# The entry of two feed-forward layers: fewer blocks of eight products, and products of later blocks between the token halves

## The chip, the cores and the metric

The kernel runs on one core of one Trainium2 chip. The metric is the device time of one execution, in microseconds (us). TensorE (PE) multiplies matrices into accumulator banks; VectorE (DVE), ScalarE (ACT) and GpSimd (POOL) work element by element; the transfers from and to HBM run through DMA queues, most of which SyncE (SP) issues. Each engine works through its own instructions in a fixed order and waits on semaphores for what the others write.

## What is computed

One step of a model of two layers, in float32, over 512 latent tokens and 128 prompt tokens. The model width is 1024, the feed-forward width 2816. The layers differ in their mixers (layer 0: two kinds of attention heads side by side, layer 1: grouped-query attention), which the change doesn't touch. What it touches is the second half of each layer:

```
g = silu(condition) @ w_mod[l] + b_mod[l]   # six vectors: shift, scale, gate of mixer and feed-forward
h = rms_norm(x, norm_ffn[l]) * (1 + scale2) + shift2
gate, up = split(h @ w_ffn_in[l])           # 1024 -> 2 x 2816
x = x + gate2 * ((silu(gate) * up) @ w_ffn_out[l])
```

Latent and prompt tokens have a condition each, so that every modulation vector is needed twice.

## The kernel before

**Operands.** The activations lie transposed, features on the 128 partitions and tokens along the free axis. The 640 tokens are two halves of 320: the first is latent, the second has 192 latent tokens and the 128 of the prompt, so that steps which depend on the condition are 192 and 128 wide there. To keep float32 precision, each operand is split into a high part and the rest (on ACT a copy, on DVE or POOL a subtraction), and a product is three matmuls: high by high, high by rest, rest by high (L61 is the line of all of them). A matmul of 128 x 128 by 320 tokens is the unit of this text.

**Feed-forward, first product.** `ffn` goes over 22 blocks of 128 hidden features. A block has a gate and an up matrix, 1024 x 128 each. It is done in one of two ways:

- *Eight products*: gate and up times both token halves, each over eight feature tiles: 2 x 2 x 8 x 3 = 96 matmuls.
- *Seven products*: the two matrices and the two token halves are cut into a 2 x 2 scheme, feature tiles 0 to 3 against 4 to 7 and half against half. With sums of weights (wX, wY, wZ, wW, made for each block, two additions of 512 for `s13` and two for `s24` among them) and sums of tokens (D, N, C, E, made once a layer by `add_up`), seven products of half the depth do the work of eight: 7 x 4 x 3 = 84 matmuls. They accumulate in three banks: fg (X times 11, then N, C, E), fd (D, then 22) and fu (X times 21). Between the products ACT copies a bank aside (p1, p5, u1) and DVE adds one; the last product (E), the SiLU and the multiplication of a block are done in `close`, after the first two products of the next block.

The first `FEW` blocks, five in layer 0 and four in layer 1, are done in the first way. The seven-product loop needs both token halves and their sums, and its weight tiles wr, w4 and ws and the tile cb serve until then as 32-bit room for the tokens (`ModS`). `hidden` splits a block's result, stores it to HBM and loads it again for the second product; the last three blocks stay.

**Second token half.** The mixer's last product adds to x column by column; its normalisation of the second half is postponed and handed to the feed-forward as `pend`, which is called after three feature tiles of block 0. It makes eight tiles h01q (layer 1: h11q) of the second half: a multiplication on DVE (h01t), a scale and shift on ACT (into h0132a, d, u), a copy on ACT (L287) and a subtraction on DVE (L288). PE reduces the squares for the norm in between (oanp, whose input is oanacc, its result oanrs).

**Second product.** It has two passes over the eight output columns n. In each column weights wo are split, PE accumulates fo, and a residual (L313) adds the gated bank to x.

**Modulation beside it.** `mod_side` makes the modulation vectors that come next: for each 128 of them a tile wm of 1024 x 128 is loaded (512 KB), and DVE multiplies it by the SiLU of either condition and sums (two `junk` steps, L1306). The conditions lie broadcast in the tile cb, which is loaded and put through SiLU once a layer. A plan, a function of the step's kind and number, says how many tiles stand behind each block ("fb") and each column ("n") of the second product.

```
side = mod_side([(0, wm0g, G2)] + [(1, wm1[j:j + 8], j) for j in (SH1, SC1, G1, SH2, SC2)],
```

These are 48 tiles in layer 0; layer 1 has the eight of its own gate.

**What sets the order.** A scheduler lays out the instructions of each engine once, when the program is built, from the order of the code and its dependences; `after` ties an instruction behind another one. Raw loads go through three buffers (`raw`, L162) on SP's queue, so that a load waits until the split of three loads before has been made; weights split by `unit` and `split` have three buffers in each of two pools.

## Time and profile before

| | us |
|---|---|
| median of three runs (least, greatest) | 1553.18 (1552.89, 1554.06) |
| span of the profiled execution | 1549.2 |
| PE busy / weight loads | 1485.5 / 1425.0 |
| DVE, ACT, POOL busy | 1109.3, 738.6, 230.0 |

HBM reads are 182.86 MB and writes 28.46 MB. The page and the rows below speak of one profiled execution; the span runs from its first to its last instruction. In a row, `out<-in` are the program's names without numbers, a time in brackets is the idle time of the engine before the instruction with what released it, and in the rows of waits the three numbers are the idle time in all, how often, and the mean. In windows the columns are the stretch, its length, and the busy time of each engine with the number of instructions; PEclk is the granted clock as a share of full speed.

### The profile page before, as it was taken

How to read it: one execution, taken by the hardware profiler on the slowest of the kernel's cores; microseconds unless marked ns; L12 is line 12 of the kernel's file. 1: busy time of each engine (PE TensorE's matmuls, PEld its weight loads, DVE VectorE, ACT ScalarE, POOL GpSimd, SP SyncE). 2: the span in 40 equal slices, each digit the busy share in tenths (PEclk: the TensorE clock that was granted, in tenths of full speed). 3: DMA queues.
4: the chain of work that ended last, by engine and by line, in shares of the span. 5: the costliest groups of instructions: out<-in, count | busy, mean ns of one | idle time of the engine just before them, and what ended most of it. 6: DMA issues, size and time to landing. Idle time of an engine off the chain costs nothing.

```text
span 1549.2 us, 25659 instructions
## 1 busy us (share of the span) xinstructions
PE 1485.5 (96%) x9988; PEld 1425.0 (92%) x9988; DVE 1109.3 (72%) x2071; ACT 738.6 (48%) x1420; POOL 230.0 (15%) x303
## 2 busy tenths in 40 slices
...
GB/s 368 109 96 169 165 140 42 14 53 125 45 210 185 176 173 160 154 238 309 232 219 133 89 41 28 28 15 96 45 199 199 160 133 136 141 219 254 88 41 69
DMA packets 73098, 212.99 MB, mean 137 GB/s; under 512 B 8096, under 2 KB 12976, under 8 KB 72720
## 3 DMA queue, kind: packets, MB, share of 16 engines
...
HBM read 182.86 MB, written 28.46 MB: 136 GB/s over the span
## 4 chain that ended last, share of the span: by engine, by line
PE 78%; DVE 11%; ACT 6%; DMA 3%; issue 2%; POOL 0%; DVEq 0%; ACTq 0%; POOLq 0%
PE fg L61 16%; PE fo L61 10%; PE fd L61 8%; PE fu L61 4%; PE gq L61 2%; PE nk L61 2%; PE nq L61 1%; PE go L61 1%; PE mod L61 1%; PE fo_2b L61 1%; PE fo_4b L61 1%; PE fo_2a L61 1%; PE fo_4a L61 1%; PE fo_6b L61 1%; PE fo_6a L61 1%
## 5 line engine op out<-in xcount | busy, mean ns | idle before, releaser
L1306 DVE SCALAR_TENSOR_TENSOR junk<-wm,cb 128x1024 bf16<-128x1024 f32 x112 | 136.7, 1221 | 25.0 <-DMA wm<-in_wm 11.2
L245 POOL TENSOR_SCALAR h10h<-h10t,gs,mods 128x320 fp32r<-128x320 f32 x4 | 5.5, 1386 | 438.9 <-DVE h10t L239 436.9
L61 PE MATMUL gq<-h10h,wgq 128*128 128x320 f32 x256 | 66.4, 318 | 0.2
L61 PE MATMUL fg<-h01q,wgu 128*128 128x320 f32 x240 | 50.2, 319 | 0.9 <-DVE h01q L288 0.4
L1069 ACT ACTIVATE wY<-s 128x1024 fp32r<-128x1024 f32 x35 | 37.1, 1060 | 23.6 <-PE fg L61 20.2
L1069 ACT ACTIVATE wZ<-s 128x1024 fp32r<-128x1024 f32 x35 | 37.1, 1060 | 23.4 <-PE fd L61 15.8
L1138 DVE TENSOR_TENSOR sg<-up,sg 128x640 f32<-128x640 f32 x35 | 28.8, 822 | 25.2 <-ACT sg L1137 25.2
L61 PEld LDWEIGHTS gq<-h10h,wgq 128*128 128x128 f32 x256 | 45.3, 190 | 1.4 <-PE gtp L65 0.6
L1070 DVE TENSOR_TENSOR wZ<-s,wZ 128x1024 fp32r<-128x1024 f32 x35 | 42.7, 1221 | 2.3
L1070 DVE TENSOR_TENSOR wY<-s,wY 128x1024 fp32r<-128x1024 f32 x35 | 42.7, 1219 | 0.5 <-ACT wY L1069 0.3
L313 DVE SCALAR_TENSOR_TENSOR xr<-fo,mods,xr 128x320 f32<-128x320 f32 (+2 forms) x48 | 19.6, 436 | 32.2 <-PE fo L61 32.0
L61 PEld LDWEIGHTS fg<-h01q,wgu 128*128 128x128 f32 x240 | 38.7, 190 | 3.6 <-DVE h01q L288 2.1
L61 PE MATMUL fg<-h11q,wgu 128*128 128x320 f32 x192 | 40.6, 320 | 0.9 <-DVE h11q L288 0.4
L1476 ACT ACTIVATE gp<-gs,gb,rq 128x640 f32<-128x640 f32 (+1 forms) x40 | 31.9, 797 | 19.2 <-DVE gb L1475 17.1
L61 PE MATMUL gq<-h10l,wgq 128*128 128x320 f32 x128 | 39.7, 310 | 0.0
L1137 ACT ACTIVATE sg<-fg 128x320 f32<-128x320 f32 x35 | 15.3, 438 | 46.7 <-PE fg L61 46.7
L61 PE MATMUL fg<-h11E,wW 128*128 128x320 f32 x216 | 34.7, 309 | 0.0
L61 PE MATMUL fd<-h11q,wZ 128*128 128x320 f32 x216 | 34.6, 309 | 0.0
L61 PE MATMUL fg<-h11q,wX 128*128 128x320 f32 x216 | 34.6, 309 | 0.0
L1171 ACT ACTIVATE p<-fd 128x320 f32<-128x320 f32 x35 | 15.3, 438 | 40.4 <-PE fd L61 40.3
L61 PE MATMUL fg<-h11N,wZ 128*128 128x320 f32 x216 | 34.6, 309 | 0.0
L61 PE MATMUL fu<-h11q,wX 128*128 128x320 f32 x216 | 34.6, 309 | 0.0
...
## 6 DMA issues: line engine op xcount, KB each, us to landing
wm<-in_wm SPq DMA_DIRECT2D x48, 512.0 KB, 4.2
mraw<-in_wm SPq DMA_DIRECT2D x24, 512.0 KB, 3.6
...
wm<-in_wm0g SPq DMA_DIRECT2D x8, 512.0 KB, 5.0
...
```

Source lines behind the costliest of these rows:

```text
L61: cls.last = nc.tensor.matmul(*a, **k)
L245: G.tensor_scalar(h[:, c0:c1], t, self.gsl[:, k, 0:1], self.ml[:, self.sh + k, 0:1], ALU.mult, ALU.add)
L313: V.scalar_tensor_tensor(xo[:, c0:c1], ps[:, c0 - o:c1 - o], ml[:, g + n, c:c + 1], xi[:, c0:c1], ALU.mult, ALU.add)
L1069: S.activation(t[:, 0, :], src, AF.Copy)
L1070: V.tensor_tensor(t[:, 1, :], src, f(t[:, 0, :]), ALU.subtract)
L1137: last = S.activation(sg[:, 0:HT], g[:, :HT], AF.Silu, scale=-1.0)
L1138: V.tensor_tensor(sg, up, sg, ALU.mult)
L1171: S.activation(p5, b5[:, :HT], AF.Copy)
L1306: V.scalar_tensor_tensor(junk, raw, 1.0, cb[:, c, :], ALU.mult, ALU.mult, accum_out=mods[l][:, j0 + i, c:c + 1])
L1476: S.activation(dst, src, AF.Exp, bias=nb, scale=rq[:, j:j + 1], accum_out=ll[:, j:j + 1])
```

## The change

- `FEW` is 2 in both layers: blocks 2, 3 and (in layer 0) 4 are done by seven products.
- `AHEAD` = 2: the first two products with wX (X times 11 and X times 21, which need only the first token half) of blocks 2 and 3 stand between block 0's first and second token half. Their sum lies in a tile p1 until the block is closed, and their gate bank stays open for N, C and E. wX_2 is loaded and split in `pre`, in the mixer's tail.
- Blocks 0 and 1 take their banks half by half, gate from one kind and up from the other, and are gated half by half. `add_up` has the first two of its four parts before the early product of block 3.
- The second half's 32-bit room takes the two w4 tiles in place of four u tiles.
- `mod_side` starts after block 1. Its load of the conditions goes through SP's queue rather than ACT's, and the SiLU is two steps of 1024, placed at block 2's close.
- The plans: layer 0 has tiles behind the blocks 6 to 21 apart from 10, 15 and 20 (13 tiles), and the second product 35 (before 16 and 32). Layer 1 has its eight tiles behind blocks 6 to 13 (before 2 to 9).

```diff
-    FEW = 5, 4
+    FEW = 2
+    AHEAD = 2
...
+            w.append(unit(wFI[l, FEW, 1], 1024, f"wX{l}_{FEW}", pool=fp))
...
+        def ahead(fb, wX):
+            g, b2, up = bank(f"fg{l}_{fb}"), bank(f"fu{l}_{fb}", "y"), utile(f"p1{l}_{fb}")
+            product(g, wX, 0, 11, True)
+            S.activation(up, g[:, :HT], AF.Copy)
+            product(b2, wX, 512, 21, True)
+            V.tensor_tensor(up, b2[:, :HT], up, ALU.add)
+            early[fb] = g, up
+
+        eight(0, w0, 0, range(3))
+        pend()
+        eight(0, w0, 0, range(3, KT))
+        wX = [w0[2]]
+        ahead(FEW, wX[0])
+        wX += [unit(wFI[l, FEW + i, 1], 1024, f"wX{l}_{FEW + i}") for i in range(1, AHEAD)]
+        w1 = [unit(wFI[l, 1, i], 1024, f"wgu{l}_1{i}") for i in range(2)]
+        sg = tmp(f"sg{l}_0")
+        gated(sg, 0)
+        for k in range(2):
+            hm.add_up(k)
+        for i in range(1, AHEAD):
+            ahead(FEW + i, wX[i])
+        eight(0, w0, 1)
...
+        step = side(fk)
...
-            after(gate, lambda: S.activation(cb, cb, AF.Silu))
...
+                if (kind, at) == ("fb", FEW):
+                    for c in range(2):
+                        S.activation(cb[:, c, :], cb[:, c, :], AF.Silu)
...
-                    lambda kind, i: (0, 0, 0, 2, 3)[i] if kind == "fb" and i < 5 else int(i % 3 > 0) if kind == "fb" else (0, 1, 1, 1, 2, 2, 2, 2, 3, 3, 3, 3, 2, 3, 2, 2)[i])
+                    lambda kind, i: int(i > 5 and i % 5 > 0) if kind == "fb" else (1, 2, 2, 2, 2, 2, 2, 2, 3, 3, 3, 3, 2, 2, 2, 2)[i])
...
-    side = mod_side([(1, wm1[G2:], G2)], lambda kind, i: int(kind == "n" or i > 1))
+    side = mod_side([(1, wm1[G2:], G2)], lambda kind, i: int(kind == "n" or i > 5))
```

**PE at the seam of the token halves, layer 0.** fg0_00 and fu0_0a are block 0's gate and up bank of the first half, h01q70 the last feature tile of that half and h01q01 the first of the second. Before:

```order
L61 MATMUL fg0_00_4883<-h01q60_4748,wgu0_0_4705 128x320 x3
L61 MATMUL fu0_0a_4885<-h01q60_4748,wgu0_1_4710 128x320 x3
L61 MATMUL fg0_00_4883<-h01q70_4749,wgu0_0_4705 128x320 x3
L61 MATMUL fu0_0a_4885<-h01q70_4749,wgu0_1_4710 128x320 x3
L61 MATMUL fg0_01_4884<-h01q01_4750,wgu0_0_4705 128x320
L61 MATMUL fu0_0b_4886<-h01q01_4750,wgu0_1_4710 128x320
```

Now (of each four feature tiles the first and the last row):

```order
L61 MATMUL fg0_00_4886<-h01q70_4752,wgu0_0_4705 128x320 x3
L61 MATMUL fu0_00_4887<-h01q70_4752,wgu0_1_4710 128x320 x3
L61 MATMUL fg0_2_4988<-h01q00_4745,wX0_2_4715 128x320 x3
...
L61 MATMUL fg0_2_4988<-h01q30_4748,wX0_2_4715 128x320 x3
L61 MATMUL fu0_2_4989<-h01q40_4749,wX0_2_4715 128x320 x3
...
L61 MATMUL fu0_2_4989<-h01q70_4752,wX0_2_4715 128x320 x3
L61 MATMUL fg0_3_5061<-h01q00_4745,wX0_3_5019 128x320 x3
...
L61 MATMUL fg0_3_5061<-h01q30_4748,wX0_3_5019 128x320 x3
L61 MATMUL fu0_3_5062<-h01q40_4749,wX0_3_5019 128x320 x3
...
L61 MATMUL fu0_3_5062<-h01q70_4752,wX0_3_5019 128x320 x3
L61 MATMUL fg0_01_5090<-h01q01_4753,wgu0_0_4705 128x320 x3
L61 MATMUL fu0_01_5091<-h01q01_4753,wgu0_1_4710 128x320 x3
```

The second half's first use stands 48 matmuls later, behind the banks fg0_2, fu0_2, fg0_3 and fu0_3.

**ACT between blocks 1 and 3, layer 0.** h01E3 is the last token sum, sg a gate's SiLU, hd0_0h the copy that a store takes, wW to wZ are splits. Before:

```order
L306 ACTIVATE h01E3_4773<-h0132d0_4736 128x320
L1294 DMA cb_4957<-in_crow 128x2048
L1122 ACTIVATE sg0_1_5211<-fg0_11_5086 128x320
L170 ACTIVATE wgu0_21_5233<-wgu0_21r_5231 128x1024
L1090 ACTIVATE hd0_0h_4251<-sg0_1_5211 128x640
L1295 ACTIVATE cb_4957<-cb_4957 128x2048
L1122 ACTIVATE sg0_2_5332<-fg0_20_5222 128x320
L170 ACTIVATE wgu0_30_5349<-wgu0_30r_5347 128x1024
```

Now:

```order
L306 ACTIVATE h01E3_4776<-h0132d0_4741 128x320
L1185 ACTIVATE wW0_2_5295<-wg0_2r_5293 128x512
L1185 ACTIVATE wW0_3_5373<-wg0_3r_5371 128x512
L1092 ACTIVATE hd0_0h_4251<-sg0_0_5032 128x640
L1336 ACTIVATE cb_5285<-cb_5285 128x1024
L1114 ACTIVATE sg0_1_5224<-fg0_11_5227 128x320
L1336 ACTIVATE cb_5285<-cb_5285 128x1024
L1092 ACTIVATE hd0_0h_4251<-sg0_1_5224 128x640
L1206 ACTIVATE p50_2_5313<-fd0_2_5310 128x320
L1071 ACTIVATE wY0_3_5379<-s130_3_5376 128x1024
L1071 ACTIVATE wX0_4_5474<-wu0_4r_5470 128x1024
L1210 ACTIVATE u10_2_5314<-fg0_2_4988 128x320
```

The load of cb has left ACT's queue, and both halves of its SiLU stand ahead of hd0_0h's second copy and of p50_2, the copy of bank fd that block 2's next product into fd waits for. On SP's queue the load stands here:

```order
L162 DMA wu0_4r_5470<-in_wFI 128x1024
L1180 DMA wg0_3r_5371<-in_wFI 128x1024
L1330 DMA cb_5285<-in_crow 128x2048
L1098 DMA sp0_0h_5170<-hd0_0h_4251 128x640
L1098 DMA sp0_0l_5172<-hd0_0l_4252 128x640
L1180 DMA wg0_4r_5472<-in_wFI 128x1024
```

It is ahead of block 0's two stores and of the loads for block 4.

**DVE at columns 3 and 4 of layer 0's second product, first pass.** xr is a column of x, wo0_0_40 and wo0_0_45 are the two weight splits of column 4, junk the modulation. Before:

```order
L313 SCALAR_TENSOR_TENSOR xr3_4486<-fo0_0_30_7965,mods0_98,xr3_4486 128x320
L1306 SCALAR_TENSOR_TENSOR junk1110_8308,mods1_99<-wm1_11_8306,cb_4957 128x1024
L1306 SCALAR_TENSOR_TENSOR junk1111_8310,mods1_99<-wm1_11_8306,cb_4957 128x1024
L313 SCALAR_TENSOR_TENSOR xr3_4486<-fo0_0_31_7966,mods0_98,xr3_4486 128x192
L313 SCALAR_TENSOR_TENSOR xr3_4486<-fo0_0_31_7966,mods0_98,xr3_4486 128x128
L1306 SCALAR_TENSOR_TENSOR junk1120_8314,mods1_99<-wm1_12_8312,cb_4957 128x1024
L1216 TENSOR_TENSOR wo0_0_50_8322<-wo0_0_50r_8320,wo0_0_50_8322 128x640
L1306 SCALAR_TENSOR_TENSOR junk1121_8316,mods1_99<-wm1_12_8312,cb_4957 128x1024
L1216 TENSOR_TENSOR wo0_0_55_8357<-wo0_0_55r_8355,wo0_0_55_8357 128x512
L313 SCALAR_TENSOR_TENSOR xr4_4553<-fo0_0_4a_8229,mods0_98,xr4_4553 128x320
L1306 SCALAR_TENSOR_TENSOR junk1130_8397,mods1_99<-wm1_13_8395,cb_4957 128x1024
L313 SCALAR_TENSOR_TENSOR xr4_4553<-fo0_0_4b_8230,mods0_98,xr4_4553 128x192
```

Now:

```order
L313 SCALAR_TENSOR_TENSOR xr3_4486<-fo0_0_30_7978,mods0_98,xr3_4486 128x320
L1344 SCALAR_TENSOR_TENSOR junk1100_8257,mods1_99<-wm1_10_8255,cb_5285 128x1024
L1344 SCALAR_TENSOR_TENSOR junk1101_8259,mods1_99<-wm1_10_8255,cb_5285 128x1024
L313 SCALAR_TENSOR_TENSOR xr3_4486<-fo0_0_31_7979,mods0_98,xr3_4486 128x192
L313 SCALAR_TENSOR_TENSOR xr3_4486<-fo0_0_31_7979,mods0_98,xr3_4486 128x128
L1344 SCALAR_TENSOR_TENSOR junk1110_8263,mods1_99<-wm1_11_8261,cb_5285 128x1024
L1252 TENSOR_TENSOR wo0_0_40_8271<-wo0_0_40r_8269,wo0_0_40_8271 128x640
L1344 SCALAR_TENSOR_TENSOR junk1111_8265,mods1_99<-wm1_11_8261,cb_5285 128x1024
L1252 TENSOR_TENSOR wo0_0_45_8306<-wo0_0_45r_8304,wo0_0_45_8306 128x512
L1344 SCALAR_TENSOR_TENSOR junk1120_8346,mods1_99<-wm1_12_8344,cb_5285 128x1024
L1344 SCALAR_TENSOR_TENSOR junk1121_8348,mods1_99<-wm1_12_8344,cb_5285 128x1024
L313 SCALAR_TENSOR_TENSOR xr4_4553<-fo0_0_4a_8267,mods0_98,xr4_4553 128x320
```

The splits of column 4 stood ahead of column 3's residuals, and those of column 5 behind a junk in that place; now it is column 4's that stand behind column 3's residuals, and two tiles of modulation lie between them.

87 lines of the change are left out of this document (47 added, 40 removed).

## The prediction

> **What bounds the kernel now.** I began with the page's first and fourth parts: what is busy, and whose work the end waits for.
>
> ```profile
> span 1549.2 us, 25659 instructions
> PE 1485.5 (96%) x9988; PEld 1425.0 (92%) x9988; DVE 1109.3 (72%) x2071; ACT 738.6 (48%) x1420; POOL 230.0 (15%) x303
> PE 78%; DVE 11%; ACT 6%; DMA 3%; issue 2%; POOL 0%; DVEq 0%; ACTq 0%; POOLq 0%
> ```
>
> TensorE (PE) sets the end; VectorE (DVE) and DMA have 14% of the chain. So a gain must be fewer matmuls or fewer waits of PE. Next I cut the feed-forward parts into stages by windows: layer 0's entry (five blocks of eight products), its seven-product loop and its second product, then layer 1's entry and loop.
>
> ```profile
> core 0: us, PE busy (x) PEld busy (x) DVE busy (x) ACT busy (x) POOL busy (x), PEclk, DMA share, GB/s
> 395.10:478.40 83.30, 77.22 (x484) 73.20 (x483) 62.97 (x116) 42.41 (x78) 2.92 (x4) 0.96 0.47 152
> 478.40:690.40 212.00, 211.45 (x1441) 210.90 (x1440) 184.01 (x269) 106.17 (x167) 0.00 (x0) 1.00 0.53 173
> 690.40:850.00 159.60, 159.60 (x1088) 159.28 (x1087) 127.92 (x230) 41.48 (x64) 9.29 (x8) 1.00 0.68 230
> 1094.00:1161.00 67.00, 61.89 (x389) 58.38 (x388) 53.42 (x101) 39.16 (x73) 2.92 (x4) 0.97 0.42 140
> 1161.00:1383.50 222.50, 222.50 (x1519) 222.39 (x1518) 176.61 (x247) 113.17 (x177) 0.00 (x0) 1.00 0.47 153
> ```
>
> The loops run without gaps: 212.00 us for 1441 matmuls is 0.147 us from start to start, so a block of 84 takes 12.35. An entry of five blocks of 96 is 480 matmuls, 70.6 us at that pace, but took 83.3; layer 1's four, 56.4, took 67.0. So 12.7 and 10.6 us are lost there. The waits of PE name part of it:
>
> ```profile
> PE fu_3a L61 <- DVE wgu L171: 4.0, 1, 4.0
> PE fu_3a L61 <- ACT wgu L170: 3.2, 1, 3.2
> PE oanp L61 <- DVE oanacc L205: 1.0, 1, 1.0
> ```
>
> Each entry has one long wait at its fourth block (fu_3a) for a split weight, the first of them in layer 0. After it the matmuls are slow:
>
> ```profile
> 449.65 3.03 PE L61 MATMUL fu_3a<-h01q,wgu 128*128 128x320 f32 x10 [4.00 <-DVE wgu L171]
> 450.00:451.00 1.00, 1.00 (x5) 1.00 (x5) 1.00 (x2) 0.18 (x1) 0.00 (x0) 0.50 0.98 343
> 454.00:455.00 1.00, 1.00 (x6) 1.00 (x5) 0.00 (x0) 0.00 (x0) 0.00 (x0) 0.52 1.02 405
> ```
>
> The clock is 0.50 from 449.65 to 455, which costs half of 5.4, 2.7 us more. Another part goes where the second token half begins:
>
> ```profile
> 402.01 2.10 DVE L281 TENSOR_TENSOR h01t<-xr,oanrs 128x320 f32<-128x320 f32 x5 [1.97 <-ACT oanrs L213]
> 403.82 0.45 ACT L287 ACTIVATE h01q<-h0132d 128x320 fp32r<-128x320 f32 x1
> 410.92 0.45 ACT L287 ACTIVATE h01q<-h0132u 128x320 fp32r<-128x320 f32 x1
> 411.67 1.04 ACT L170 ACTIVATE wgu<-wgu_10r 128x1024 fp32r<-128x1024 f32 x1
> 412.62 0.46 ACT L287 ACTIVATE h01q<-h0132u 128x320 fp32r<-128x320 f32 x1
> ```
>
> ScalarE (ACT) makes one of the half's eight tiles per (410.92 - 403.82) / 6 = 1.18 us; PE uses one in 6 x 0.147 = 0.88. The last is copied at 413.1, its rest split 0.5 and multiplied 0.9 later: some 10.3 us from the first tile's 404.3 where 7.06 would do, 3.2 lost. Together 1.0 + 3.2 + 4.0 + 2.7 = 10.9 of the 12.7 us.
>
> **The change, part by part.** *Fewer products.* Three blocks of layer 0 and two of layer 1 go from 96 matmuls to 84: 5 x 12 x 0.147 = 8.8 us less for PE.
>
> *Second token half.* PE has two early products (48 matmuls, 7.06 us) before it needs that half. What delays the half: three weight splits (wX_3, both of block 1) now stand on DVE ahead of its first multiply. A split costs DVE 1.13 and ACT 0.95, a 320-wide step 0.40, by the distances of these starts and of 411.67 to 412.62; steps of 512 and 640 lie between by their size, 0.60 and 0.74:
>
> ```profile
> 413.07 1.22 DVE L171 TENSOR_TENSOR wgu<-wgu_10r,wgu 128x1024 fp32r<-128x1024 f32 x1
> 414.20 0.49 DVE L288 TENSOR_TENSOR h01q<-h0132u,h01q 128x320 fp32r<-128x320 f32 x1
> 414.61 1.22 DVE L171 TENSOR_TENSOR wgu<-wgu_11r,wgu 128x1024 fp32r<-128x1024 f32 x1
> 384.21 0.55 DVE L313 SCALAR_TENSOR_TENSOR xr<-oa,mods,xr 128x320 f32<-128x320 f32 x1 [1.89 <-PE oa L61]
> ```
>
> DVE's wait of 1.97 us at 402.01 covers most of the 3.4, so the first multiply starts at 403.5. The half's last tile follows 2.3 (402.0 to 404.3) + 7 x 1.18 + 0.4 (one copy of a bank on ACT) later, at 414.5. PE: from 395.1 the first half takes 7.06, the norm 0.4, a wait for the norm 1.4 (1.0 as before, and 0.4 because wX_3's split stands ahead of its last addition) and one for the last tile 0.4: 404.4. The early products end at 411.5, and the last tile is wanted at 417.7: no wait, 3 us to spare. The half ends at 418.5, block 1 at 432.6. The split of wX_2 is new in the mixer's tail, where DVE waits 1.89 us for PE; I cost it at nothing, and without that cover it is 1.1.
>
> *Sums and weights for block 2.* They have lost the time of three blocks. From 403.5 DVE has 16 steps of the half, 32 of the sums and 5 on banks (53 x 0.40 = 21.2), five half-wide steps (3.0), a store's split (0.74) and two splits (2.26): 27.2 us, ready at 430.7, where PE wants them at 432.6. Hidden by 1.9 us; beyond that each microsecond is one of PE.
>
> *Conditions.* Their load goes from ACT's queue to SP's, behind the load of wg_3; behind it stand block 0's stores and wg_4, wanted a block later. On ACT the first half of their SiLU stands ahead of block 1's last gate, the second ahead of the store's copy and of p_2, which block 2's third product waits for.
>
> ```profile
> 425.84 0.47 ACT h01D L306
> 427.04 8.66 DMA cb<-in_crow
> 435.72 1.91 ACT cb L1295
> 1126.07 0.33 ACTq L1294 DMA_DIRECT2D cb<-in_crow  x1
> 1133.18 1.92 ACT L1295 ACTIVATE cb<-cb 128x2048 f32<-128x2048 f32 x1 [3.62 <-DMA cb<-in_crow]
> ```
>
> The room that it lands in is read last at about 425.8, as before, so it lands 8.7 us on, at 434.5 (layer 1: 7.1 us, 1.6 sooner). Then 0.95 + 0.4 + 0.95 + 0.6 + 0.4: p_2 at 437.8. PE has done its two products at 432.6 + 3.5 = 436.1: a wait of 1.7, and 0.6 more for u_2 behind two splits. Layer 1: 0.1 + 0.6. Bounds: none of it, or the load 4 us later and 2.7 for the clock in each layer.
>
> *Sum of an entry.* Blocks 0 to 3 are 2 x 96 + 2 x 84 = 360 matmuls, 52.9 us; with 0.4 + 1.4 + 0.4 and 2.3 (0.7) that is 57.4 and 55.8. Then 18 blocks in both layers, 222.3. Before: 83.3 + 17 x 12.35 = 293.2, and 67.0 + 222.3 = 289.3. Gains: 293.2 - 279.7 = 13.5 and 289.3 - 278.1 = 11.2, together 24.7.
>
> *Modulation in the loop.* 13 tiles stand in blocks 6 to 21 of layer 0 (four blocks of five), 8 in blocks 6 to 13 of layer 1. A block costs DVE three splits, five half-wide steps, three of 0.40 and two of 0.74, 9.1 us; a tile's two products 2.4; together 11.5 of 12.35. Windows of one block each say that DVE can be fuller without holding PE up:
>
> ```profile
> 478.40:490.70 12.30, 12.30 (x84) 12.07 (x83) 12.27 (x19) 7.35 (x10) 0.00 (x0) 1.00 0.63 191
> 490.70:503.00 12.30, 12.30 (x86) 12.30 (x85) 11.73 (x20) 6.67 (x11) 0.00 (x0) 1.00 0.50 157
> DVE s L1157 <- DMA wg_11r<-in_wFI: 2.1, 1, 2.1
> ```
>
> I take 0; above it, 6 us if the waits for loads of wg (up to 2.1) remain in some blocks.
>
> *Modulation in layer 0's second product.* Its first eight columns now have 15 tiles instead of 11, so the weight splits come later in DVE's order: column 4's stands behind column 3's residual and a junk, column 5's behind column 4's likewise, column 6's behind a residual and a small addition. PE gets no further than two matmuls without it.
>
> ```profile
> 721.03 0.67 DVE L313 SCALAR_TENSOR_TENSOR xr<-fo,mods,xr 128x192 f32<-128x192 f32 x2
> 721.62 1.22 DVE L1306 SCALAR_TENSOR_TENSOR junk<-wm,cb 128x1024 bf16<-128x1024 f32 x1
> 722.76 0.82 DVE L1216 TENSOR_TENSOR wo<-wo_50r,wo 128x640 fp32r<-128x640 f32 x1
> 728.67 7.91 PE fo L61 x54
> ```
>
> Before, the same three steps stood there, but the split was column 5's, which PE reached 5 us later, at 728.67. Now PE waits 0.1 + 0.6 + 1.15 + 0.8 less two matmuls, 2.4 us, at columns 4 and 5, and 1.2 at column 6: 6.0. Bounds: 0 if DVE is ahead of the columns; 12 if loads come late too (a load of wm takes 4.2) or the clock drops.
>
> ```profile
> wm<-in_wm SPq DMA_DIRECT2D x48, 512.0 KB, 4.2
> 861.00:864.00 3.00, 3.00 (x10) 2.34 (x9) 1.11 (x3) 2.00 (x4) 0.81 (x1) 0.52 0.01 4
> PE gkp L61 <- ACT ksq L1372: 3.0, 1, 3.0
> 400.00:402.00 2.00, 1.90 (x11) 1.74 (x12) 0.05 (x1) 1.00 (x2) 1.33 (x2) 1.00 0.03 8
> ```
>
> Whether it drops: after gkp's wait of 3.0 us it was 0.52, after oanp's of 1.0 us, at 400, it stayed 1.00. My 2.4 lie between and nearer the 3.0, but short of it; I price no drop and keep one as a rival. The Trainium skill's page "TensorE: Matmul & The Clock Gate" (Part 1) puts the drop at an idle window of about 3.4 us, by which my sum would stay and the rival (b) would fall away. This trace has it after 3.0 already, so the page's limit is too kind here and the rival keeps its chance.
>
> **Sum.** 24.7 less 6.0 is 18.7 us. The span 1549.2 becomes 1530.5. The median of the runs, 1553.18, lies 4.0 above the profiled span; with that, 1534.5.
>
> **Rivals.** (a) *DVE is early enough in the second product*, and the waits at columns 4 to 6 don't come: 24.7 us, 1528.5. For it: DVE was busy in only 127.92 of 159.60 us there. Against: in DVE's fixed order these splits follow a residual that waits for PE.
> (b) *The clock drops* after the waits at columns 4 and 5 and after layer 0's wait for p_2: 3 x 2.7 = 8.1 us come back, 1542.6. For it: 3.0 us were enough. Against: no wait of mine reaches 3.0.
> (c) *DVE becomes the pace of the loop*, the case on the other side: in each of the 21 blocks with a tile, 11.5 and a wait for wg of 2.1 exceed 12.35 by 1.25, in all 26 us, 7.6 more than is gained: 1560.5. It decides from 18.7 / 21 = 0.9 us a block on. For it: DVE's waits for wg. Against: such waits shrink when DVE comes later, and 12.27 busy held nobody.
> (d) *The early products don't cover the half*: the gate bank of the second half is the one that the first half's SiLU must empty, which on ACT stands behind the last tile's copy and a table load of the SiLU: about 415.8 where PE is ready at 411.5, and with the clock's 2.7 7.0 us in each layer, less the 3.0 for p_2 and u_2 that it covers: 11.0, so 1545.5. Against: of four such banks the norm's is free much sooner.
>
> **How the numbers follow.** Forecast 0.58, (a) 0.12, (b) 0.12, (c) 0.12, (d) 0.06. About 0.2% (3.1 us) is what a measurement can tell from no change; (c) lands within it between 0.74 and 1.04 us a block, to which I give 0.05 of its 0.12. Faster: 0.58 + 0.12 + 0.12 + 0.06 = 0.88; the same 0.05; slower 0.07. The range reaches over (a) and (b) and takes 3 us on either side for the waits of the entries and the loop: 1525 to 1546.
>
> **What would show it.** 60 matmuls fewer, and PE's waits at fu_3a gone. Right: in layer 0 some 57 us from the first fg matmul to the end of four blocks' worth of products, a wait of about 2 us in block 2 for p, and about 2.4 at fo_4a and the column after it, at clock 1.00. Wrong: a gap between the early products and the second half (d); waits of PE for wX, wY, wZ or g in blocks 6 to 21 (c); a clock near 0.5 in the second product (b). If fo_4a doesn't wait, (a).

## The result, and the profile after

The change takes 1537.64 us (median of four runs, 1536.04 to 1539.75) beside 1553.04 for the kernel before on the same chip (1552.67 to 1554.06): the medians lie 15.4 us apart. The ratio estimated from all these runs is 0.9908, with a 95% interval of 0.9891 to 0.9924, which is 14.3 us less (11.8 to 16.9). Run again with the experiments it took 1536.31 beside 1551.49, a ratio of 0.9902 (0.9882 to 0.9921).

The page of the changed kernel, its first and fourth parts:

```profile
span 1537.9 us, 25619 instructions
PE 1468.7 (96%) x9928; PEld 1411.5 (92%) x9928; DVE 1139.1 (74%) x2115; ACT 749.1 (49%) x1447; POOL 231.9 (15%) x303
PE 71%; DVE 14%; DMA 7%; ACT 5%; issue 3%; POOL 0%; POOLq 0%; DVEq 0%; SPq 0%; ACTq 0%
```

The 60 matmuls are gone (9988 to 9928), and PE is busy 16.8 us less. Yet DMA has 7% of the chain where it had 3%: some of the waits that ended are replaced by others.

The stages in windows of the changed kernel: layer 0's entry (blocks 0 and 1 and the two blocks that follow, 360 matmuls, up to block 4's first matmul with the sum D), its loop to the last product E, its second product; then layer 1's entry and loop.

```profile
core 0: us, PE busy (x) PEld busy (x) DVE busy (x) ACT busy (x) POOL busy (x), PEclk, DMA share, GB/s
396.06:452.28 56.22, 53.88 (x365) 53.20 (x364) 55.62 (x104) 40.90 (x80) 3.97 (x4) 1.00 0.47 153
452.28:681.41 229.13, 224.63 (x1522) 222.84 (x1521) 193.99 (x285) 112.17 (x178) 0.00 (x0) 1.00 0.52 167
681.41:843.36 161.95, 156.55 (x1051) 155.30 (x1050) 135.78 (x241) 36.76 (x54) 3.70 (x4) 0.99 0.72 242
1093.23:1149.45 56.22, 53.88 (x365) 53.20 (x364) 55.61 (x104) 40.89 (x80) 3.98 (x4) 1.00 0.46 152
1149.45:1372.37 222.92, 222.60 (x1519) 222.23 (x1517) 183.85 (x261) 113.43 (x178) 0.00 (x0) 1.00 0.49 158
```

The kernel before (layer 0 from its first feed-forward matmul to the first matmul with the sum D, which stands behind five blocks there; the second product):

```profile
395.11:480.26 85.15, 79.07 (x497) 75.06 (x495) 64.82 (x119) 43.86 (x80) 2.92 (x4) 0.96 0.46 149
690.10:844.12 154.02, 154.02 (x1051) 153.86 (x1050) 122.77 (x221) 37.29 (x55) 3.57 (x4) 1.00 0.70 235
```

From its first feed-forward matmul to the last E, layer 0 took 295.0 us before (395.11 to 690.10) and takes 285.4 now; its second product 154.0 and 162.0; layer 1 289.3 and 279.1. So the two profiles differ by -9.6, +7.9 and -10.2, and with +0.95 ahead of layer 0's entry and -0.4 in other places by 11.3. The medians differ by 15.4, because the profiled run of the change was 2 us slower than its median and that of before some 2 us quicker than its own: in every run here about 1.85 us lie between the span and the time (1539.75 against 1537.9), which puts the execution of 1549.2 at about 1551. In what follows stages are compared, since the unchanged mixer ahead of layer 0's entry moves by up to 7 us between profiles.

PE's waits in the changed kernel, with idle time in all, how often, and the longest (the third number is the longest, not the mean, in the prediction's rows of waits too):

```profile
PE fg L61 <- ACT u L1210: 4.8, 7, 1.1
PE fo L61 <- DVE wo L1252: 2.1, 1, 2.1
PE fo_4a L61 <- DVE wo L1252: 1.4, 1, 1.4
PE fg L61 <- POOL h01q L291: 1.2, 1, 1.2
PE oanp L61 <- DVE oanacc L205: 1.1, 1, 1.1
PE fo_6a L61 <- DVE wo L1252: 1.0, 1, 1.0
```

The waits at fu_3a, 7.2 us in the kernel before, are gone. The entries keep a little over 2 us each: oanp, and the last tile of the *first* token half (h01q, in layer 1 h11q, whose rest POOL makes behind DVE's split of wX_3). New are seven waits at u, six of them in layer 0's loop and one in layer 1's, and four waits in layer 0's second product.

**The loop's waits.** Rows of one round of layer 0's loop: DVE, then SP's issues, then PE's wait. The work runs ahead of itself: the load is that of block 18, the split of wW that of block 17, and PE is at the last product of block 16.

```profile
605.81 0.69 DVE L1188 TENSOR_TENSOR s<-wg_18r 128x512 f32<-128x512 f32 x1 [1.89 <-DMA wg_18r<-in_wFI]
...
608.16 1.22 DVE L1344 SCALAR_TENSOR_TENSOR junk<-wm,cb 128x1024 bf16<-128x1024 f32 x1
...
609.91 1.22 DVE L1344 SCALAR_TENSOR_TENSOR junk<-wm,cb 128x1024 bf16<-128x1024 f32 x1
...
611.79 0.68 DVE L1186 TENSOR_TENSOR wW<-wg_17r,wW 128x512 fp32r<-128x512 f32 x1
...
599.69 0.43 SPq L1180 DMA_DIRECT2D wg_18r<-in_wFI  x1
...
612.66 0.33 SPq L1098 DMA_DIRECT2D sp_15h<-hd_0h  x1
613.04 0.42 SPq L1180 DMA_DIRECT2D wg_19r<-in_wFI  x1
...
613.02 2.03 PE L61 MATMUL fg<-h01C,wY 128*128 128x320 f32 x12 [0.78 <-ACT u L1210]
```

This is a closed chain. The load of wg_18 has landed 6.1 us after its issue (599.69 to 605.81); DVE, which sat idle for it, goes through s, wY, two junks and others to the split of wW; only that split frees a buffer of the wg loads, and the next one is issued at 613.04, behind a store. From issue to issue 13.35 us, where PE needs 12.31 for a block. The store, the bank copies and u all hang on the same DVE steps, and so PE waits up to 1.1 us at u. From block 11 to block 18 PE loses 6.15 us, in layer 1 0.58. The kernel before had the chain too: its loads of wg from the 11th on are 14.5, 11.3, 11.9, 13.3, 11.5, 12.1 and 13.4 us apart. There every third block had no tile and caught up.

**The second product's waits.** ACT, DVE and PE at column 4 of the changed kernel:

```profile
712.30 0.74 ACT L1251 ACTIVATE wo<-wo_40r 128x640 fp32r<-128x640 f32 x1 [7.76 <-DMA wo_40r<-in_wFO]
...
712.71 0.67 DVE L313 SCALAR_TENSOR_TENSOR xr<-fo,mods,xr 128x192 f32<-128x192 f32 x2
713.29 1.21 DVE L1344 SCALAR_TENSOR_TENSOR junk<-wm,cb 128x1024 bf16<-128x1024 f32 x1
...
714.43 0.82 DVE L1252 TENSOR_TENSOR wo<-wo_40r,wo 128x640 fp32r<-128x640 f32 x1
...
713.09 0.41 PE L61 MATMUL fo_4a<-hd_1h,wo 128*128 128x320 f32 x1 [0.95 <-ACT wo L1251]
...
715.31 0.64 PE L61 MATMUL fo_4a<-hd_1h,wo 128*128 128x320 f32 x1 [1.37 <-DVE wo L1252]
```

As foreseen, column 4's split of wo on DVE stands behind column 3's residual and a junk. The first of the two waits (0.95) has another cause: ACT's split waited for its load, which was issued only at 708.88, when a junk had freed its buffer. In all this cost nothing more, since DVE's split would have held PE until 715.3 in either case. From start to start of the matmuls (less 0.147 each) PE loses 1.1, 1.5 and 0.3 us at column 4, 2.2 at column 5 and 1.2 at column 6: 6.3 us. The other 1.7 is the clock:

```profile
715.00:717.00 2.00, 1.69 (x6) 1.69 (x7) 2.00 (x4) 0.00 (x0) 0.00 (x0) 0.52 0.99 361
717.00:718.50 1.50, 1.50 (x8) 1.50 (x7) 0.00 (x1) 0.00 (x0) 0.00 (x0) 0.50 1.02 407
718.50:720.00 1.50, 1.50 (x12) 1.50 (x11) 0.56 (x1) 0.00 (x0) 0.00 (x0) 1.00 1.01 376
```

It is 0.50 from 715.1 to 718.5 (eight matmuls in 1.5 us, then twelve in as long).

### The profile page after: what moved, and what is told of

Read it like the earlier page. It is cut to its first block, busy times and chain, and to the rows that moved or that the text cites. A ratio compares the mean times of both kernels' runs of the same rounds, so it can differ in the third digit from the quotient of the medians.

```text
span 1537.9 us, 25619 instructions
## 1 busy us (share of the span) xinstructions
PE 1468.7 (96%) x9928; PEld 1411.5 (92%) x9928; DVE 1139.1 (74%) x2115; ACT 749.1 (49%) x1447; POOL 231.9 (15%) x303
## 4 chain that ended last, share of the span: by engine, by line
PE 71%; DVE 14%; DMA 7%; ACT 5%; issue 3%; POOL 0%; POOLq 0%; DVEq 0%; SPq 0%; ACTq 0%
PE fg L61 14%; PE fo L61 10%; PE fd L61 6%; PE fu L61 5%; PE gq L61 2%; PE nq L61 2%; DVE junk L1344 2%; PE nk L61 2%; DMA wm<-in_wm 1%; PE fo_4a L61 1%; PE go L61 1%; PE fo_2b L61 1%; PE fo_0b L61 1%; PE fo_0a L61 1%; PE mod L61 1%
## 5 line engine op out<-in xcount | busy, mean ns | idle before, releaser
L1344 DVE SCALAR_TENSOR_TENSOR junk<-wm,cb 128x1024 bf16<-128x1024 f32 x112 | 136.6, 1219 | 10.8 <-DMA wm<-in_wm 10.1
L1071 ACT ACTIVATE wY<-s 128x1024 fp32r<-128x1024 f32 x40 | 42.4, 1060 | 21.4 <-PE fg L61 21.1
L1072 DVE TENSOR_TENSOR wZ<-s,wZ 128x1024 fp32r<-128x1024 f32 x40 | 48.8, 1219 | 1.3
L1071 ACT ACTIVATE wZ<-s 128x1024 fp32r<-128x1024 f32 x40 | 42.3, 1056 | 14.6 <-PE fd L61 12.7
L1072 DVE TENSOR_TENSOR wY<-s,wY 128x1024 fp32r<-128x1024 f32 x40 | 48.8, 1219 | 0.2
L61 PE MATMUL fg<-h01C,wY 128*128 128x320 f32 x240 | 39.1, 311 | 4.5 <-ACT u L1210 4.5
L61 PEld LDWEIGHTS fg<-h01C,wY 128*128 128x128 f32 x240 | 35.7, 188 | 6.1 <-ACT u L1210 6.1
L61 PE MATMUL fg<-h11C,wY 128*128 128x320 f32 x240 | 38.5, 309 | 0.3 <-ACT u L1210 0.3
L61 PE MATMUL fg<-h01E,wW 128*128 128x320 f32 x240 | 38.6, 309 | 0.0
L61 PE MATMUL fd<-h01q,wZ 128*128 128x320 f32 x240 | 38.4, 309 | 0.0
L61 PE MATMUL fg<-h01N,wZ 128*128 128x320 f32 x240 | 38.4, 309 | 0.0
```

Source lines behind the costliest of these rows:

```text
L61: cls.last = nc.tensor.matmul(*a, **k)
L1071: S.activation(t[:, 0, :], src, AF.Copy)
L1072: V.tensor_tensor(t[:, 1, :], src, f(t[:, 0, :]), ALU.subtract)
L1344: V.scalar_tensor_tensor(junk, raw, 1.0, cb[:, c, :], ALU.mult, ALU.mult, accum_out=mods[l][:, j0 + i, c:c + 1])
```

## The experiments

Differences in time are to the kernel before on the same chip (1551.69, 1552.48, 1551.49 or 1550.9 us), unless the changed kernel is named. These medians spread by some 2 us from chip to chip, so that a difference of that size between runs of different chips says nothing; the stages of the profiles say more.

**The change once more.** No edit.

> Edit: none, the change itself beside the others on the same chip. Expected 1535 to 1540, the loop of layer 0 with 4 to 7 us of waits for u and its second product 160 to 163 us from the last E product on.

1536.31 us (1535.48 to 1538.05), ratio 0.9902 (0.9882 to 0.9921). Stages: 284.4, 160.5 and 278.6, which is 10.6 less, 6.5 more and 10.7 less than before. In the second product PE waits as in the first profile (1.2, 1.5 and 0.3 at column 4, 1.9 at 5, 1.2 at 6), but the clock stays at full speed, and the whole price is 6.5.

**Modulation later in the second product.** The first column gets no tile, the first pass 11 as in the kernel before, and the second pass takes the rest.

```diff
-                    ... else (1, 2, 2, 2, 2, 2, 2, 2, 3, 3, 3, 3, 2, 2, 2, 2)[i])
+                    ... else (0, 1, 1, 1, 2, 2, 2, 2, 3, 3, 3, 3, 3, 3, 3, 3)[i])
```

> Edit: the second product of layer 0 gets its 35 modulation tiles as 0,1,1,1,2,2,2,2 and then three at each of the eight columns of the second pass (the change has 1 and seven times 2 in the first pass). In the profile of the change that second product takes 165.0 us instead of 157.8; PE waits 2.4 us at fo_4a, 2.1 at column 5 and 1.0 at fo_6a, and the clock is halved for 3.4 us from 715 us on (1.7 lost). Theory A (the weight splits stand behind the modulation in DVE's order): the first pass loses its waits, second product about 158, time 7.2 us under the change's 1537.6, about 1530.5; the four more tiles in the second pass are hidden. Rival B (the weights' loads come late, held up by tiles that share the raw buffers): as many tiles in all, so the waits only move to the second pass and the time stays within 2 us of 1537.6.

1535.15 us (1532.79 to 1537.51), 0.9885 (0.9866 to 0.9904). The second product took 160.0, hardly less than the repeat's 160.5. The waits at columns 4 and 5 are gone, and others came in the second pass; of PE's waits in this kernel:

```profile
PE fn0p L61 <- DVE mods L1348: 1.0, 1, 1.0
PE fo L61 <- DVE wo L1252: 1.0, 1, 1.0
```

fn0p is the norm at the end of the layer. With 35 tiles, moving some from the first pass to the second moved the waits: 3.4 us are left of 6.3. After the one at fo the clock was 0.50 from 818.9 to 822.3, which is 1.7 more of the 160.0 us, and the repeat had no such drop. The place in the order was named rightly, and taking it away did not win the 6 us. By the time rival B is nearer than theory A; of its reason, late loads, the rows show little (one wait of 0.4 us for a split on ACT that waited 0.3 us for its load). (The expectation's 165.0 and 157.8 us are cut at other events than the 162.0 and 154.0 above.)

**The junks behind the split of wW.** No plan is changed; the two products of a tile are tied behind wW's split of the block two later, so that they leave the closed chain.

```diff
-            step("fb", fb)
+            if fb < FEW + 2:
+                step("fb", fb)
...
-            V.tensor_tensor(wW[1], rg[:, 512:], f(wW[0]), ALU.subtract)
+            wl = V.tensor_tensor(wW[1], rg[:, 512:], f(wW[0]), ALU.subtract)
+            if fb > FEW + 3:
+                after(wl, lambda: step("fb", fb - 2))
...
+        for fb in (FB - 2, FB - 1):
+            step("fb", fb)
```

> Edit: the modulation of a block is put behind the split of wW of the block after next (in DVE's order behind sg and wW instead of ahead of both); the amount of work is the same. In the profile of the change six blocks of layer 0's loop and one of layer 1's take 12.9 to 13.7 us instead of 12.3, with PE waiting for u: 6.2 and 0.6 us. Theory A (a closed chain: wW's split frees the buffer that wg's load waits for, the load lands 6.1 us later, and s, wY, two junks and sg stand between it and the next wW, 13.3 us in all): with the junks outside this chain it is 10.9, all blocks take 12.3, time about 6.8 us under the change's 1537.6, about 1531. Rival B (DVE simply has too much to do in a block with a tile): the same sum of work, so the waits stay, 1537 to 1538.

1533.32 us (1530.12 to 1538.1), 0.9875 (0.9852 to 0.9897). The window of layer 0's loop:

```profile
453.79:678.04 224.25, 222.78 (x1520) 222.51 (x1519) 196.47 (x285) 113.75 (x178) 0.00 (x0) 1.00 0.54 173
```

From block 4 on, every block of layer 0 takes 12.31 or 12.32 us, with the same 13 tiles, and DVE is busier in a shorter loop (196.47 us against 193.99). So the loop's 6 us were the chain and not DVE's total work. The loop is 4.9 us shorter and not 6, since the last E comes 1.3 us later behind the last D than in the change (14.9 against 13.6). Layer 1 paid some of it back: 281.2 against 279.1, with 1.1 us in blocks 12 to 14, where eight tiles stand in a row, and 1.6 at block 2, where the load of the conditions took 8.0 us and PE waited for p (0.9 us). The intervals of the two ratios overlap, so that the whole kernel is not shown to be faster than the change.

**No early products.** The two early products are left out; blocks 2 and 3 are done like the others of the loop.

```diff
-    AHEAD = 2
+    AHEAD = 0
-            w.append(unit(wFI[l, FEW, 1], 1024, f"wX{l}_{FEW}", pool=fp))
...
-        ahead(FEW, wX[0])
```

> Edit: two blocks of eight products as in the change, but no early products; blocks 2 and 3 take all their seven in order. PE has the same matmuls. The scheduler puts some of block 1's first-half products among block 0's second half. Theory A (the early products cover the second half's lateness and the sums for block 2; in the change the half's last tile is split 3.1 us, and wY_2 2.3 us before PE wants them): PE arrives 7.0 us sooner and waits 3 to 5 us in each entry, part of it long enough to halve the clock, 6 to 12 us over the change's 1537.6. Rival B (fewer products alone bring the gain, and the order among the token halves matters little since the scheduler fills the gap): within 2 us of 1537.6.

1543.10 us (1540.56 to 1546.04), 0.9936 (0.9918 to 0.9953): its median is 5.5 above the change's, though the intervals just meet. But the entry was not where it was lost. Windows of the mixer's tail ahead of layer 0's entry and of the entry:

```profile
333.83:399.07 65.24, 62.70 (x413) 61.21 (x412) 36.64 (x67) 23.53 (x40) 12.83 (x8) 0.97 0.30 97
399.07:455.00 55.93, 53.95 (x365) 53.20 (x364) 55.24 (x102) 40.96 (x80) 3.91 (x4) 1.00 0.45 149
```

The entry is as long as the change's 56.22, with as many matmuls. DVE in the tail:

```profile
384.79 1.23 DVE L1071 TENSOR_TENSOR wX<-wu_2r,wX 128x1024 fp32r<-128x1024 f32 x1 [4.58 <-ACT wX L1070]
385.93 0.54 DVE L313 SCALAR_TENSOR_TENSOR xr<-oa6a,mods,xr 128x320 f32<-128x320 f32 x1
```

The tail took 65.24 us against 61.07 in the change: DVE sits 4.58 us at a split of the loop's first block, which the scheduler put ahead of the mixer's own residual, and the norm waits for that (PE's wait at oanp, 2.5 us). In layer 1 the tail is 1.9 longer in the same way. So this run could not say what the products are worth, and the next one separates them from the split.

**No early products, but wX_2 split early as in the change.**

```diff
-    AHEAD = 2
+    AHEAD = 0
...
-            if fb not in early:
-                wX = split(ru, f"wX{l}_{fb}")
+            wX = w0[2] if fb == FEW else split(ru, f"wX{l}_{fb}")
```

> Edit: as e3 (two blocks of eight, no early products), but wX_2 is loaded and split in the mixer's tail at the place where the change has it, and block 2 uses it from there. In e3 the entry from the first fg matmul to the last of the 22 blocks took 283.6 us with 4.4 us of loop waits, so the same as the change's 285.4 with 6.2; its loss stood ahead of the entry, where PE waits 2.7 us for the first half's norm (the split of wu_2, whose load comes late, stands ahead of the residuals on ACT and DVE) and the clock is halved. Theory A (inside the entry the early products bring nothing that the scheduler's filling with block 1's products doesn't bring): the tail is whole again and the time is within 2 us of the change's 1537.6. Rival B (they cover the second half): 3 to 6 us over it, with PE waits for h01q or wY_2.

1532.76 us (1530.67 to 1533.82), 0.9876 (0.9856 to 0.9895). The tail and the second product:

```profile
336.10:397.18 61.08, 61.08 (x413) 60.06 (x412) 35.98 (x66) 23.06 (x38) 13.00 (x8) 1.00 0.35 113
680.81:836.84 156.03, 154.11 (x1048) 153.43 (x1047) 125.55 (x227) 37.18 (x55) 3.57 (x4) 1.00 0.71 237
```

The tail is whole again (61.08, no idle PE). Layer 0 to the last E took 283.6 us and layer 1 278.9, the repeat of the change 284.4 and 278.6; without the loops' waits (3.1 and 5.1 us in layer 0) the early products are worth 1.2 us in layer 0 and 0.3 in layer 1. Left to itself the scheduler puts first-half products of block 1 in their place. That the time is 3.5 below the repeat's is the second product's doing, 156.0 against 160.5 with the same 35 tiles: here two junks stand earlier and column 4's split ahead of column 3's second residual. The two ratios' intervals overlap, so that the whole kernel is not shown to be faster.

**Four blocks of eight products.** The change with `FEW` = 4, whose blocks 1 to 3 all go half by half.

```diff
-    FEW = 2
+    FEW = 4
...
+        for fb in range(1, FEW):
+            wf = w1 if fb == 1 else [unit(wFI[l, fb, i], 1024, f"wgu{l}_{fb}{i}") for i in range(2)]
+            for c in range(2):
+                eight(fb, wf, c)
...
```

> Edit: four blocks of eight products in both layers, with the early products of blocks 4 and 5 between the halves of block 0; the rest as in the change. 24 matmuls more in each layer, 48 x 0.147 = 7.1 us. Theory A (the old wait at fu_3a, 4.0 and 3.2 us and the halved clock after it, came from the order around the second half and is gone with it): 7.1 us over the change's 1537.6, about 1544.7. Rival B (that wait comes from the weights: a block of eight needs two new split matrices in 14 us while DVE has the sums, so the third and fourth block wait again): up to 10.9 us more on top, 1548 to 1556, with PE waits at fg or fu for wgu.

1546.92 us (1545.22 to 1550.34), 0.9966 (0.9953 to 0.9979): 9.3 slower than the change's first median. 48 matmuls are 7.0 us. PE's longest wait for a weight of these blocks is 0.6 us, so the long wait at fu_3a didn't come from the fourth block of eight as such; the rest of the price came in layer 1, where two blocks of the loop take 13.8 and 13.2 us.

**Only fewer blocks of eight.** The kernel before, with one number changed.

```diff
-    FEW = 5, 4
+    FEW = 2, 2
```

> Edit: the kernel before with two blocks of eight products in both layers, and nothing else of the change (no early products, conditions and modulation where they were; their plan's tiles of blocks 3 and 4 now stand behind blocks of seven). 60 matmuls fewer, 8.8 us. Theory A (the old wait of 4.0 and 3.2 us at fu_3a came from the conditions' load on ACT's queue and the modulation that stand there, so fewer products alone only move it): block 2's and 3's products wait in its place, and the gain is 0 to 9 us, 1544 to 1553. Rival B (it belonged to the fourth block of eight): it goes away too, with the halved clock behind it, 8.8 + 10.9 = 19.7 us, 1533.

1543.14 us (1540.89 to 1544.6), 0.9944 (0.9926 to 0.9963): 8.5 us less, where the 60 matmuls are worth 8.8. From the first feed-forward matmul to the last E layer 0 gains 10.3 and layer 1 4.7 (the entries alone 12.0 and 4.7), and 6.1 are lost in the two mixer tails (4.0 and 2.1) as without the early products above: PE waits 2.1 us at oanp. In the change the early split of wX_2 is what keeps the tails whole.

**Only the conditions and the modulation later.** The kernel before, with five and four blocks of eight; its conditions go through SP's queue, their SiLU is in two steps at block 5's close, and the plans are the change's.

```diff
-            nc.scalar.dma_start(cb, ...)
-            after(gate, lambda: S.activation(cb, cb, AF.Silu))
+            nc.sync.dma_start(cb, ...)
...
+                if (kind, at) == ("fb", 5):
+                    for c in range(2):
+                        S.activation(cb[:, c, :], cb[:, c, :], AF.Silu)
...
```

> Edit: the kernel before with five and four blocks of eight and no early products, but with the change's third part alone: the load of cb on SP's queue, its SiLU in two steps placed at block 5's close, and the change's plans. The entry is read from the trace: from the first fg matmul to the first fd matmul 85.2 us in layer 0 and 68.7 in layer 1 before. Theory A (conditions and modulation held up the weights of the fourth block): PE's waits at fu_3a fall under 1 us and the entries are 5 to 11 us shorter together. Rival B (DVE's sums and the second half's lateness hold them up): entries within 2 us of before. In the time the plans' price in the loop and in layer 0's second product (up to 6.8 and 7.3 us in the change) stands against it: by A 1545 to 1555, by B 1555 to 1567.

1552.64 us (median of ten runs, 1549.94 to 1556.92), 1.0009 (0.9993 to 1.0024): no difference. Two large terms cancel. Windows from the first feed-forward matmul to the first with D in layers 0 and 1, and of the second product:

```profile
394.51:473.03 78.52, 76.46 (x496) 72.64 (x495) 56.33 (x104) 44.12 (x82) 2.92 (x4) 1.00 0.42 137
1093.88:1158.40 64.52, 62.19 (x400) 58.55 (x399) 49.87 (x95) 40.74 (x77) 2.91 (x4) 1.00 0.39 137
688.64:844.68 156.04, 154.12 (x1048) 153.44 (x1047) 125.44 (x227) 37.18 (x55) 3.57 (x4) 1.00 0.71 238
```

PE's wait in the two loops:

```profile
PE fg L61 <- ACT u L1175: 7.3, 12, 0.9
```

The entries gain 6.6 (85.15 to 78.52) and 4.2 (68.71 to 64.52), with the long waits at fu_3a gone (0.3 us is left) and the clock at 1.00. What stood ahead of block 3's two weight splits in layer 0 of the kernel before is in the rows of ACT and, from 445 on, of DVE:

```profile
435.72 1.91 ACT L1295 ACTIVATE cb<-cb 128x2048 f32<-128x2048 f32 x1 [5.20 <-DMA cb<-in_crow]
...
437.86 1.05 ACT L170 ACTIVATE wgu<-wgu_30r 128x1024 fp32r<-128x1024 f32 x1
...
445.56 1.23 DVE L1306 SCALAR_TENSOR_TENSOR junk<-wm,cb 128x1024 bf16<-128x1024 f32 x1 [2.58 <-DMA wm<-in_wm0g]
...
448.38 1.22 DVE L171 TENSOR_TENSOR wgu<-wgu_31r,wgu 128x1024 fp32r<-128x1024 f32 x1
```

ACT sat 5.20 us for the conditions, took 1.9 for their SiLU, and the first of block 3's weight splits stood behind it. The second, wgu_31, is the one that fu_3a waited for until 449.65; on DVE two tiles of modulation stand ahead of it, and the second of them waited 2.58 us for its load. The run moves the conditions and these tiles together, so that their shares are not separated. The loops then lose 10.4 us (5.7 and 4.7), most of it in the twelve waits at u: the chain of the loop, with tiles in four blocks of five, and in layer 1 in eight in a row. The second product loses 2.0.

**The order of the loop and other plans.** The change with the junks behind wW as above; layer 0 with 16 tiles in the loop and 32 in the second product as in the kernel before; layer 1 with a tile in every other block.

```diff
+            if fb > FEW + 3:
+                after(wl, lambda: step("fb", fb - 2))
...
-                    lambda kind, i: int(i > 5 and i % 5 > 0) if kind == "fb" else (1, 2, 2, 2, 2, 2, 2, 2, 3, 3, 3, 3, 2, 2, 2, 2)[i])
+                    lambda kind, i: int(i > 3 and i % 9 > 0) if kind == "fb" else (0, 1, 1, 1, 2, 2, 2, 2, 3, 3, 3, 3, 2, 3, 2, 2)[i])
...
-    side = mod_side([(1, wm1[G2:], G2)], lambda kind, i: int(kind == "n" or i > 5))
+    side = mod_side([(1, wm1[G2:], G2)], lambda kind, i: int(kind == "n" or (i > 4 and i % 2 > 0)))
```

> Edit: the change, with the modulation behind wW's split (as in e2), 16 tiles in layer 0's loop (blocks 4 to 21 without 9 and 18), the second product's 32 tiles as in the kernel before, and layer 1's eight tiles at blocks 5, 7 to 19 in turn. Theory A (loop and second product cost 6.8 and 7.9 us in the change only through the places of the modulation): both go, 14.7 us under the change's 1537.6, about 1523. Rival B (more tiles in the loop fill DVE: a block with a tile takes it 12.6 us in the trace of e2 where eight stand in a row): the loop of layer 0 waits again by 0.3 us in each of 16 blocks, up to 5 us, about 1528.

1526.48 us (1525.32 to 1533.23) beside 1551.69, ratio 0.9847 (0.9826 to 0.9868): 25.2 us below the kernel before, the fastest kernel of the study. Layer 0's loop and second product:

```profile
457.15:681.47 224.32, 223.50 (x1524) 222.97 (x1523) 202.96 (x298) 112.52 (x178) 0.00 (x0) 1.00 0.55 177
681.47:836.51 155.04, 154.11 (x1050) 153.69 (x1049) 128.69 (x228) 36.89 (x54) 3.69 (x4) 1.00 0.73 243
```

The second product takes 155.0 against 162.0 and 160.5, and the loop, with three tiles more, leaves PE idle for 0.8 us. Both new waits of the change can thus be had away without giving back the entries (layer 0 280.5, layer 1 278.5).

**The same plans without the edit of the order.**

> Edit: e7's plans without its order, that is the change with 16 tiles in layer 0's loop (blocks 4 to 21 without 9 and 18), 32 in the second product and layer 1's at every other block. Theory A (the closed chain of e2: a block with a tile takes 13.3 us, 0.95 too long, a block without one catches up 1.4; in the change 13 tiles with two useful rests cost 6.2, so 3.4 us are to spare at first): 16 x 0.95 - 2 x 1.4 - 3.4 = 9.0 us of waits for u in layer 0's loop and none in layer 1's, against none in e7, so 9 us over e7's 1526.5, 1535. Rival B (the order doesn't matter with rests placed so): within 2 us of 1526.5.

1528.23 us (1527.45 to 1531.74), 0.9852 (0.9832 to 0.9873). My theory had the waits in the loop come back, and they did not: 281.5 us for layer 0, with 1.6 us of waits at the loop's end, and 155.2 for the second product. The rival, that the plans alone do it, holds. The traces show why. In the change both junks stand between DVE's first step on a new wg and wW's split in ten of layer 0's blocks (by the number of wW 7, 10 to 13 and 15 to 19), and a run of such blocks goes at 13.3 us each. With tiles from block 4 on instead of 6 the scheduler itself laid the junks elsewhere, and only five blocks (14, 15, 16, 18, 19) have both there, the others one or none. At about 0.95 us each, less some 3.3 us by which DVE is ahead by then, 1.5 is what one would expect. That last estimate was made afterwards from this run and is not tested by another.

**Splits behind the first half's last tile.** The kernel with the order and the new plans, and in it the splits of wX_3 and of block 1's weights tied behind the first half's last tile, against the waits at oanp and h01q.

```diff
-        wX += [unit(wFI[l, FEW + i, 1], 1024, ...) for i in range(1, AHEAD)]
-        w1 = [unit(wFI[l, 1, i], 1024, f"wgu{l}_1{i}") for i in range(2)]
+        wX += [after(hm.act[7, 0], lambda: unit(wFI[l, FEW + i, 1], 1024, ...)) for i in range(1, AHEAD)]
+        w1 = [after(hm.act[7, 0], lambda: unit(wFI[l, 1, i], 1024, f"wgu{l}_1{i}")) for i in range(2)]
```

> Edit: e7, and the splits of wX_3 and of block 1's weights are tied behind the last tile of the first token half. In the change (and e7) PE waits 1.2 us in each layer for that tile, whose multiply stands behind the 1.9 us split of wX_3 on DVE, and 1.2 for the norm. Theory A (only DVE's order): both waits shrink, 2 to 4 us under e7's 1526.5, about 1523. Rival B (the three splits then delay the second half and the sums, which had 2 to 3 us to spare): as much comes back at block 2, 1525 to 1529.

1534.21 us (1530.44 to 1535.6), 0.9885 (0.9867 to 0.9904): not faster, and its median is 7.7 above that of the kernel that it was made from, which ran on another chip; the intervals of the two ratios just meet. By stages layer 0 takes 1.6 and layer 1 3.0 us more to the last E. The wait at h01q is gone in both layers, and oanp keeps 1.0. But now the wait for p that I had predicted for the change itself is there. PE's wait:

```profile
PE fd L61 <- ACT p L1209: 5.7, 2, 3.0
```

ACT's rows ahead of it in layer 0:

```profile
434.82 2.00 ACT L1341 ACTIVATE cb<-cb 128x1024 f32<-128x1024 f32 x2 [3.47 <-DMA cb<-in_crow]
436.73 0.72 ACT L1092 ACTIVATE hd_0h<-sg 128x640 fp32r<-128x640 f32 x1
437.35 0.41 ACT L1209 ACTIVATE p<-fd 128x320 f32<-128x320 f32 x1
```

ACT sits 3.47 us for the conditions, and p_2 stands behind them: 5.7 us in the two layers.

**The same with the SiLU of the conditions behind block 3's u.**

```diff
-            S.activation(u1, g[:, :HT], AF.Copy)
+            uact = S.activation(u1, g[:, :HT], AF.Copy)
+            if fb == FEW + 1:
+                after(uact, lambda: step("cb", 0))
...
-                if (kind, at) == ("fb", FEW):
+                if kind == "cb":
```

> Edit: e9 with the SiLU of the conditions put behind block 3's copy u (in the change and e9 it stands ahead of block 2's p). In e9 PE reaches block 2's third product 3 us sooner than in the change and then waits 3.15 and 2.93 us for p, which stands on ACT behind this SiLU and so behind the load of cb. Theory A (the conditions' landing is the next bound of the entry): these waits go, the entry to block 4 takes 53.5 instead of 56.4 us in both layers, 5 to 6 us under e7's 1526.5, about 1521. Rival B (weights or sums of block 2 are no earlier than the conditions): PE waits as long for wY, wZ or the sums, 1525 to 1528.

1530.02 us (1527.43 to 1533.71), 0.9855 (0.9831 to 0.9879). Neither theory: the SiLU is out of the way, and PE still waits 2.4 us for p (2.2 in layer 1). ACT's row ahead of p at that place:

```profile
439.59 0.74 ACT L1092 ACTIVATE hd_0h<-sg 128x640 fp32r<-128x640 f32 x1 [4.73 <-DMA sp_0h<-hd_0h]
```

Ahead of p stands the copy of block 1's result, which waits until block 0's store has left the same tile. That store was issued 1.0 us behind the load of the conditions (430.03 and 431.04) and took 8.5 us; in the change, issued 2.5 us behind it, 2.9. So the load delayed p by two ways, through ACT and through the store, and taking away the first uncovered the second. Another room for that copy was not tried.

## Why the prediction was right or wrong

The forecast of 1534.5 is 3.1 us below the measured 1537.64, which lies in its range; faster was right. Against the profiled execution 18.7 us of gain were forecast; 15.4 are measured between the medians, and 18.7 is outside the interval of 11.8 to 16.9. Between the two profiled executions the gain is 11.3, so that part of the nearness is luck (the last point below). Term by term:

| term | forecast | measured |
|---|---|---|
| entries, layer 0 and 1 | 13.5 + 11.2 = 24.7 | 14.9 + 10.7 = 25.6 |
| loop of layer 0 and 1 | 0 (up to 6) | -6.15 - 0.58 = -6.7 |
| end of layer 0's loop | 0 | +0.9 |
| second product of layer 0 | -6.0 | -7.9 (-6.5 in the repeat) |
| from the span to the median | +4.0 | +1.85 |

Layer 0's entry went from 83.4 us (85.15 less twelve matmuls) to 56.2 and one block of 12.3; layer 1's from 66.95 to 56.2. The +0.9 are short waits of the old loop and its end.

- **Entries: right, by partly other waits.** Four blocks' worth took 56.2 us in either layer, forecast at 57.4 and 55.8. The early products covered the second half: its last tile was split at 416.1 and wanted at 419.7, the forecast had 3 us to spare; rival (d) did not come. The sums and, last of block 2's operands, wY_2 were ready 2.3 us ahead. The wait for the last tile of the first half cost 1.2 instead of 0.4.
- **The conditions: wrong step.** "so it lands 8.7 us on, at 434.5" failed. On SP's queue the load was issued at 427.87 and landed 4.6 us later. The 8.7 us were those of a load issued 1.2 us behind one of wg; in the change that distance is 2.4 us (the last section has all such loads). These rows of ACT in the change have p before PE asks for it:

```profile
432.50 1.06 ACT L1336 ACTIVATE cb<-cb 128x1024 f32<-128x1024 f32 x1 [2.13 <-DMA cb<-in_crow]
...
436.64 0.44 ACT L1206 ACTIVATE p<-fd 128x320 f32<-128x320 f32 x1 [0.19 <-PE fd L61]
```

  p waits for PE and not PE for it: the 2.3 and 0.7 us didn't come, and this made up for the larger waits at the tiles. That the mechanism was real shows where the entry is shortened further (5.7 us for p in the two layers, above), and in layer 1 of the run with the junks behind wW, where the load took 8.0 us and PE waited 0.9 us for p. So it was in part luck that this wait stayed away.
- **Where the gain comes from.** Of the 25.6 us 8.8 are the 60 matmuls. Fewer blocks of eight alone shorten the entries by 16.7 us, waits included, and the later place of conditions and modulation alone, in the kernel before, by 10.8; the two sum to 27.5, so they overlap, and how the waits divide between them is open. The early products bring 1.5 us at most. Their split of wX_2 has another use: without it 6 us are lost in the mixers' tails.
- **The loop: the step that failed.** "I take 0; above it, 6 us if the waits for loads of wg (up to 2.1) remain in some blocks." They remained, and the price was the bound, not the value taken. The reason against it, in rival (c), "such waits shrink when DVE comes later", is what fell. They would if the load came by itself; it waits for DVE's own split of wW, so a later DVE makes a later load, and 6.1 us of landing stay in the chain at each block. The "12.27 busy" that "held nobody" was one block of a plan with a rest in every third. Rival (c) added up the right two terms, DVE's steps and its wait for wg: 1.05 us a block (13.36 against 12.31) where it had 1.25. But it charged all 21 blocks, and only seven of layer 0's and one of layer 1's lost time, after what DVE was ahead had been used up. Its sign was named wrongly too: PE waited for u, and not for wX, wY, wZ or g. The junks behind wW, with the same DVE work, took the waits away, which shows the chain and not DVE's load as the cause.
- **The second product: place right, size a little low.** Columns 4, 5 and 6 waited for their splits in the order foreseen: 2.9, 2.2 and 1.2 against 2.4, 2.4 and 1.2. The clock, priced at no drop, halved once for 3.4 us in the first profile (1.7 us of rival (b)'s 8.1) and not in the repeat; in three of the experiments with the same waits at column 4 it halved too. The argument that the 15 tiles of the first eight columns cause it was too narrow: with 11 there and 35 in all the waits came later, with 32 in all they are gone but for one of 0.9 us, and with the same 35 in another DVE order 156.0 was reached, without the early products as in the kernel before with the change's plans. It is a backlog of DVE and its order, not the count in the first pass alone.
- **The offset.** The 4.0 us between span and median were the 1.85 or so that lie between in each run, and 2 by which the profiled execution was quick. That this execution was no typical one could be seen in nothing that the page shows; the forecast was helped by it, since 1530.5 and 1.85 alone would have been 1532.4. The waits that the loop and the second product had over the forecast were 8.6 us in the first profile; 1.8 us more of gain in the entries and at the loop's end, the quick profile of before (2.1) and the slow one of the change (2.1) hid most of that.
